# The last gate columns and the fifth chunk's second turn behind the down group, with fixed places for the late gates

## The chip, the core and the metric

The kernel runs on one core of a Trainium2 chip. The engines named here are PE (matrix products, written to PSUM banks), DVE and ACT (work on tiles of 128 rows), POOL, and SP, which here issues nearly all transfers. Each engine works through its own queue in order and waits where an operand is not yet there. The metric is the time of one execution on the device in microseconds (us); the time of the kernel before is the median of its runs, 891.66 us (891.43 to 891.97).

## The reference, cut to what matters

The input is a sequence of 256 rows of width 1024. Two layers follow, each of them a feed-forward part (FFN), a mixer and a second FFN; the first layer's mixer is a convolution module, the second's a latent attention (MLA). All of it is in 32-bit floats.

```
def swiglu_ffn(h, w1, w3, w2):
    return (jax.nn.silu(h @ w1) * (h @ w3)) @ w2          # w1, w3: 1024 x 2816, w2: 2816 x 1024

for i in range(DEPTH):                                     # DEPTH = 2
    h = h + 0.5 * swiglu_ffn(rmsnorm(h, ffn_norm1[i]), ffn1_w1[i], ffn1_w3[i], ffn1_w2[i])
    h = h + mixer(rmsnorm(h, mix_norm[i]))                 # conv module, then MLA
    h = h + 0.5 * swiglu_ffn(rmsnorm(h, ffn_norm2[i]), ffn2_w1[i], ffn2_w3[i], ffn2_w2[i])
return rmsnorm(h, final_norm)
```

There are thus four FFNs, called FFN0 to FFN3 below, and they run one after the other with the mixers between them: FFN0, conv, FFN1, FFN2, MLA, FFN3.

## The kernel before, in words

**Products in three parts.** A 32-bit product is made of three products in a faster format: each operand is split into a high part (a rounded copy, made by ACT for weights: `hi`, L248 and L216) and a low part (what is left, made by DVE: `lo`, L249 and L202), and PE adds hi·lo, hi·hi and lo·hi into one bank (`mm3`, L334, L337, L338). One such product of 128 x 128 by 128 x 512 starts about every 0.227 us on PE.

**Weights.** The weights come as raw blocks of 1 MB (128 x 2048) through SP's queue, in the order in which they are used (L240 for most, L225 and L182 for those loaded ahead of a mixer or of the next FFN). Four raw buffers take turns, so a load starts once the block four places earlier has been split by both ACT and DVE. Each block is split in two halves (128 x 1024). Five buffers hold the split blocks.

**An FFN, up part.** The gate columns are made in chunks: five chunks of 512 columns of w1 and w3 and a sixth, half as wide, whose w1 and w3 columns lie in one block (`both` in the code, c = 5). A chunk's products `u` stand in four PSUM banks of tag A (two for each half of the 256 rows, tb = 0, 1); the sixth chunk has two. ACT takes the Silu of the w1 products (L1005), DVE multiplies by the w3 products (L1011) and gives `s`, which is silu(h w1) · (h w3) for 128 rows and 512 columns. The fourth chunk is made by a scheme of seven products in place of eight ("seven"), with added and subtracted blocks.

**The turn of the gates.** The down product needs the gates with the columns on the partitions. So each `s` is turned: DVE transposes it in 32 x 32 pieces (STREAM_TRANSPOSE, L505, `gt<-s`), SP writes it to memory in four transfers of 64 KB (L509, `gd<-gt`), and reads it back with one of 256 KB (L514, `gb<-gd`); ACT then makes the high half Gh (L890; L881 for the last columns) and DVE the low half Gl (same lines). `turn` does so for chunks 0 to 4, `turn_last` for the sixth chunk, whose two halves share one tile.

**The down part.** The 22 column blocks of the gates are used in pairs, so w2 has 11 blocks, counted 0 to 10. Blocks 0 to 3 are used by a second group of seven products (`seven_products`, with casts L216 and L202, sums L260 and forms L367/L370), then blocks 4 to 8 one after another (`Rows.block`, each 24 products for all four output banks), and the last two in `Rows.finish`, bank by bank. Where the FFN is followed by a norm that is turned by transfers (`apart`: FFN1 and FFN2), `finish` takes the last three, blocks 8 to 10. The gates of the last columns belong to blocks 9 and 10 and those of the fifth chunk to blocks 8 and 9.

**Hand-over.** As each output bank is done, DVE adds it to h (L826). From FFN0 to conv the norm's scaled rows `hn` (L707, L708) are transposed on PE (`tp`, L473); from FFN1 to FFN2 and from FFN2 to MLA the rows of h are turned by transfers like the gates (`hd<-rows` L509, `rows<-hd` L514) and then split into Xh (ACT, L625) and Xl (DVE, L626).

**What sets the order.** The program is written in the order of the code, and a scheduler places each engine's instructions by priority; `urgent` raises it, and `order(a, b)` puts a behind b with no wait of its own where both are on one engine. So a call of `order` between instructions of one engine fixes their places in its queue. `casts[n, i]` is the pair (hi, lo) of half i of the n-th block; `n_used[0]` counts the blocks used; `last_turn[0]` is the latest transpose; `gates` lists the pairs (Gh, Gl).

Of the kernel before, what the change touches and what calls it, by code (L numbers as in the profile page):

```python
# [19 lines left out]
P = 128  # L20
# [69 lines left out]
def trunk(ctx: ExitStack, tc: tile.TileContext, x, xt, first, pos, invf, gfin, wdw,  # L90
# [283 lines left out]
    def seven_products(xh, xl, forms, banks, late={}, ahead=False):  # L374
# [30 lines left out]
        kept = tmp.tile([P, 512], F32, tag="s", name=uid("p5"))  # L405
# [376 lines left out]
    class Rows:  # L782
# [6 lines left out]
        def seven(self, forms, late):  # L789
            seven_products(self.zh, self.zl, forms, self.o, late)  # L790
# [17 lines left out]
        def finish(self, rh, make_next, act, apart=False):  # L808
# [62 lines left out]
    def ffn_in(act, X, make_next, beside, apart, seven_up, seven_down):  # L871
        down_sums, first_form = [], {}
# [55 lines left out]
        for c in range(6):  # L928
# [18 lines left out]
            for m in range(0 if u else 1 if both else 2):  # L947
# [4 lines left out]
                for tb in range(NT):  # L952
                    u[m, tb] = bank("A", "u")
# [42 lines left out]
            if both:  # L996
                last_s = tmp.tile([P, 512], F32, tag="s", name=uid("s"))
            for tb in range(NT):
                if both:
                    s = last_s.rearrange("p (f t c) -> p t f c", t=NT, c=P)[:, tb]  # L1000
                    ug, uu = (u[0, tb][:, v].rearrange("p (f c) -> p f c", c=P) for v in (slice(w), slice(w, 2 * w)))
                else:
                    s = tmp.tile([P, 512], F32, tag="s", name=uid("s"))
                    ug, uu = u[0, tb], u[1, tb]
# [5 lines left out]
                mul = urgent(nc.vector.tensor_mul) if c in seven_up or c + 1 in seven_up else nc.vector.tensor_mul  # L1010
                mul(s, s, uu)  # L1011
                if not both:
                    turn(c, tb, w, s)
        o = Rows(Gh, Gl, NF, make_next is Final, seven_down)
        if seven_down:
            both = (xp.tile([P, KT, S], F32R, tag=tag, name=uid("rows")) for tag in ("Xh", "Xl"))
            late = {2: None, 3: None}
            o.seven({**first_form, **forms_of(down_sums[1:], *both, late)}, late)
            turn_last(last_s)
            for gate in gates[-NT - 2:]:  # L1020
                for ins, cast in zip(gate, casts[n_used[0] + 1, 0]):
                    order(ins, cast.ins)
        stage.append("down")
        for i in range(4 if seven_down else 0, NF // 2 - (3 if apart else 2)):
            beside()
            o.block(i)
            beside()
# [876 lines left out]
```

## Time and profile before

| What | us |
|---|---|
| median of the runs (lowest, highest) | 891.66 (891.43, 891.97) |
| the profiled execution, its own time | 891.0 |
| its span in the profile | 889.1 |
| PE busy | 881.5 (99%) |
| DVE busy | 768.7 (86%) |
| ACT busy | 580.2 (65%) |
| POOL busy | 104.8 (12%) |

Times in the rows are counted from the span's start. A row of a timeline has the start, the duration, the engine, the line, the operation, the output and the inputs by tile name, the shape, the count where neighbours of one kind are drawn together, and in brackets how long the engine sat idle before and what ended that. SPq rows are the times at which SP issues a transfer; a tile's answer has the time from issue to landing (least, median, most). The windows about the down parts' ends (busy time of each engine, its instructions, the granted clock as a share, the share of the transfer engines that was in use, GB/s) are:

```profile
core 0: us, PE busy (x) PEld busy (x) DVE busy (x) ACT busy (x) POOL busy (x), PEclk, DMA share, GB/s
143.00:181.00 38.00, 38.00 (x174) 31.54 (x172) 30.50 (x51) 30.85 (x68) 0.95 (x3) 1.00 0.83 307
405.00:446.00 41.00, 41.00 (x183) 33.95 (x182) 29.93 (x34) 22.30 (x32) 1.18 (x4) 1.00 0.88 327
579.00:620.00 41.00, 41.00 (x183) 33.95 (x182) 29.81 (x34) 22.35 (x31) 0.95 (x3) 1.00 0.83 305
840.00:884.00 44.00, 43.15 (x202) 36.04 (x200) 28.67 (x34) 21.30 (x31) 1.48 (x5) 1.00 0.43 165
```

They are FFN0, FFN1, FFN2 and FFN3 in this order.

### The profile page before, as it was taken

The page shows a single profiled execution, that of the slowest core. Times are in us where ns is not written, and L with a number is a line of the kernel's source. Part 1 is how long each engine was busy: PE and PEld are TensorE (multiplying, and loading weights), DVE is VectorE, ACT ScalarE, POOL GpSimd, SP SyncE. Part 2 cuts the span into 40 slices and gives each one's busy share as a digit, 9 for nine tenths or more (in the row PEclk, how much of TensorE's full clock was granted, in tenths as well). Part 3 has the DMA queues.
Part 4 walks back from the last instruction along what each step waited for, and adds up shares of the span by engine and source line. Part 5 has one row for each costly group of instructions (what it writes and reads, how often), then busy time and mean ns, then how long its engine had stood idle before and what let it go on. Part 6 is the DMA issues. An engine that isn't in the chain of part 4 may idle for free.

```text
span 889.1 us, 12241 instructions
## 1 busy us (share of the span) xinstructions
PE 881.5 (99%) x4209; PEld 741.9 (83%) x4209; DVE 768.7 (86%) x1106; ACT 580.2 (65%) x1001; POOL 104.8 (12%) x227
## 2 busy tenths in 40 slices
PE   9999999999999999999999999999999999999997
PEld 7888887898988888888888888888899888888886
DVE  6899999789999899989598999995778679999873
ACT  7667858789887656647385465673777666563762
POOL 1000000079952000000010000001400010000000
PEclk9999999999999999999999999999999999999999
DMA  9884929834216945929859278396644558387451
GB/s 336 302 312 148 390 84 354 330 137 148 96 60 230 328 188 204 360 83 358 293 191 335 93 259 308 116 394 200 224 144 142 190 171 334 99 324 257 160 218 48
DMA packets 68174, 198.94 MB, mean 224 GB/s; under 512 B 7952, under 2 KB 38544, under 8 KB 48784
## 3 DMA queue, kind: packets, MB, share of 16 engines
q1 hardware_dynamic: 67680, 197.47, 62.4%
q8 instruction: 33, 0.54, 0.2%
q10 hardware_dynamic: 432, 0.69, 0.2%
q14 instruction: 29, 0.24, 0.1%
HBM read 181.87 MB, written 16.25 MB: 223 GB/s over the span
## 4 chain that ended last, share of the span: by engine, by line
PE 97%; DVE 1%; ACT 0%; DMA 0%; issue 0%; ACTq 0%
PE u L338 17%; PE u L334 17%; PE u L337 17%; PE o L334 9%; PE o L338 9%; PE o L337 9%; PE u L1060 3%; PE gate L1060 3%; PE o L1296 3%; PE u L438 2%; PE sc L1657 1%; PE tp L473 1%; DVE lo L202 1%; PE pairs L1103 1%; PE a L337 1%; PE a L338 1%
## 5 line engine op out<-in xcount | busy, mean ns | idle before, releaser
L249 DVE TENSOR_TENSOR lo<-raw,hi 128x1024 fp32r<-128x1024 f32 (+1 forms) x228 | 267.0, 1212 | 25.8 <-ACT hi L248 25.2
L248 ACT CAST hi<-raw 128x1024 fp32r<-128x1024 f32 (+1 forms) x230 | 229.1, 1044 | 83.9 <-DMA raw<-in_f2w 31.5
L338 PE MATMUL u<-hi,Xl 128*128 128x512 f32 x592 | 230.4, 389 | 0.0
L337 PE MATMUL u<-hi,Xh 128*128 128x512 f32 x592 | 230.3, 389 | 0.0
L334 PE MATMUL u<-lo,Xh 128*128 128x512 f32 x592 | 229.8, 389 | 0.0
L216 ACT CAST hi<-raw 128x1024 fp32r<-128x1024 f32 x112 | 111.5, 1050 | 59.7 <-DVE raw L202 44.8
L202 DVE TENSOR_TENSOR lo<-raw,hi 128x1024 fp32r<-128x1024 f32 x112 | 132.1, 1216 | 2.5 <-ACT hi L216 2.4
L338 PEld LDWEIGHTS u<-hi,Xl 128*128 128x128 f32 x592 | 111.1, 188 | 23.5 <-DVE Xl L492 0.5
L337 PEld LDWEIGHTS u<-hi,Xh 128*128 128x128 f32 x592 | 111.1, 188 | 23.1
L334 PEld LDWEIGHTS u<-lo,Xh 128*128 128x128 f32 x592 | 111.1, 188 | 23.0
L337 PE MATMUL o<-hi,Gh 128*128 128x512 f32 (+1 forms) x276 | 106.5, 386 | 0.0
L338 PE MATMUL o<-hi,Gl 128*128 128x512 f32 (+1 forms) x276 | 106.5, 386 | 0.0
L334 PE MATMUL o<-lo,Gh 128*128 128x512 f32 (+1 forms) x276 | 106.2, 387 | 0.0
L464 POOL TENSOR_TENSOR ms<-ss 128x1 f32<-128x1 f32 x16 | 8.1, 510 | 592.6 <-ACT junk L456 592.6
L202 DVE TENSOR_TENSOR raw<-raw,raw 128x2048 f32<-128x2048 f32 x32 | 73.2, 2288 | 2.4 <-DMA raw<-in_f1w 1.2
L334 PEld LDWEIGHTS o<-lo,Gh 128*128 128x128 f32 x276 | 51.8, 188 | 10.7 <-DVE lo L202 0.2
L337 PEld LDWEIGHTS o<-hi,Gh 128*128 128x128 f32 x276 | 51.8, 188 | 10.4
L338 PEld LDWEIGHTS o<-hi,Gl 128*128 128x128 f32 x276 | 51.8, 188 | 10.4
L1005 ACT ACTIVATE s<-u,R 128x512 f32<-128x512 f32 (+1 forms) x48 | 30.6, 647 | 36.3 <-PE u L338 35.4
L1149 DVE SCALAR_TENSOR_TENSOR acc<-V,dw,acc 128x128 f32<-128x128 f32 (+1 forms) x174 | 53.9, 392 | 0.0
L1170 ACT ACTIVATE prod<-V,dw 128x128 f32<-128x128 f32 (+1 forms) x128 | 45.6, 415 | 1.8 <-POOL Y L1171 1.0
L826 DVE SCALAR_TENSOR_TENSOR h<-o,rh,h 128x512 f32<-128x512 f32 (+1 forms) x18 | 13.0, 720 | 27.2 <-PE o L338 27.2
(271 smaller groups left out, 1303.8 us busy)
## 6 DMA issues: line engine op xcount, KB each, us to landing
raw<-in_f2w SPq DMA_DIRECT2D x66, 1024.0 KB, 6.0
raw<-in_f1w SPq DMA_DIRECT2D x62, 1024.0 KB, 7.0
raw<-in_cw SPq DMA_DIRECT2D x12, 1024.0 KB, 6.2
gd<-gt SPq DMA_DIRECT2D x176, 64.0 KB, 3.8
gb<-gd SPq DMA_DIRECT2D x28, 256.0 KB, 3.3
rows<-gd SPq DMA_DIRECT2D x16, 256.0 KB, 3.0
raw<-in_wo SPq DMA_DIRECT2D x4, 1024.0 KB, 4.8
hd<-rows SPq DMA_DIRECT2D x56, 64.0 KB, 2.3
```

The source lines that it names most:

```text
L202: ins = nc.vector.tensor_sub(out, left, right)
L216: casts[n, i] = nc.scalar.copy(hi[:, c], raw[:, c]), sub(lo[:, c], raw[:, c], hi[:, c].bitcast(F32))
L248: casts[len(loaded), i] = (nc.scalar.copy(hi[:, c], raw[:, c]), low.tensor_sub(lo[:, c], raw[:, c], hi[:, c].bitcast(F32)))
L249: low.tensor_sub(lo[:, c], raw[:, c], hi[:, c].bitcast(F32)))
L334: mm = nc.tensor.matmul(o, ah, bl, start=start, stop=False, skip_group_check=seeded)
L337: nc.tensor.matmul(o, ah, bh, start=False, stop=False, skip_group_check=seeded)
L338: return nc.tensor.matmul(o, al, bh, start=False, stop=stop, skip_group_check=seeded)
L1005: silu = nc.scalar.activation(s, ug, AF.Silu, scale=X.r[tb])
L1060: mm = nc.tensor.matmul(u[:, t], w[:, c], X.x[:, k, t], start=(k == 0), stop=(k == KT - 1))
L1149: dve_last.append(nc.vector.scalar_tensor_tensor(out if j == j1 - 1 else y, v, w, y, op0=ALU.mult, op1=ALU.add))
L1170: prods_last.append(nc.scalar.activation(p, v, AF.Copy, scale=w))
L1296: p = nc.tensor.matmul(o[tb, d], (Zl if kind == "x" else Zh)[:, f, tbs(tb)], (lo if kind == "l" else hi)[:, c], start=(f, kind) == (0, "l" ...
```

## The change

1. The sixth chunk's products `u` go to banks of tag B in place of A.
2. The sixth chunk's Silus, products and turn, and the fifth chunk's second turn (c = 4, tb = 1), are written behind the down part's seven group. Their places are fixed: the fifth chunk's second transpose behind the lo of block 4, the Silus behind the hi of block 4, the products behind the lo of block 5, and block 6's lo behind the last transpose.
3. The gates of the last four turns are ordered behind the second half of block 5's casts (before: those of the last columns and the three ahead of them behind block 5's first half), and the last two gates, on ACT and on DVE, behind block 7's casts and ahead of block 8's.
4. `kept`, the copy of the second product in the seven group, uses the rows tile of the first sum instead of a tile of `tmp`.
5. In `finish` the first product of a bank is ordered behind the last product of the bank ahead of it.

The number of instructions on PE, DVE, ACT, POOL and SP stays as it was. The core of the diff:

```
-    def forms_of(sums, sh, sl, late={}):
+    def forms_of(sums, sh, sl, late={}, after=None):
...
+            if i == 0 and after is not None:
+                order(cast, after.ins)
...
-        kept = tmp.tile([P, 512], F32, tag="s", name=uid("p5"))
+        if kept is None:
+            kept = tmp.tile([P, 512], F32, tag="s", name=uid("p5"))
...
                         after = nxt.turned if i == 3 and a == 1 and rh is not None and not self.last else ()
+                        if rh is not None and i and a == 0:
+
+                            after = done,
...
         def turn_last(g):
 
             bv = turn_blocks(act, g, 4, "g", ())
-            order(last_turn[0], casts[n_used[0], PIECES - 1][1].ins)
...
-                    u[m, tb] = bank("A", "u")
+                    u[m, tb] = bank("B" if both else "A", "u")
...
-            if both:
-                last_s = tmp.tile([P, 512], F32, tag="s", name=uid("s"))
-            for tb in range(NT):
...
-                silu = nc.scalar.activation(s, ug, AF.Silu, scale=X.r[tb])
-                if both and seven_down and tb == 0:
-                    load_to(n_used[0] + 3)
-                    for i in range(PIECES):
-                        order(casts[n_used[0] + 2, i][0], silu.ins)
...
+            for tb in range(0 if both else NT):
+                s = tmp.tile([P, 512], F32, tag="s", name=uid("s"))
+                nc.scalar.activation(s, u[0, tb], AF.Silu, scale=X.r[tb])
+                mul = urgent(nc.vector.tensor_mul) if c in seven_up or c + 1 in seven_up else nc.vector.tensor_mul
+                mul(s, s, u[1, tb])
+                if 2 * c + tb < 9:
+                    turn(c, tb, w, s)
                 else:
...
+                    late_turns.append((c, tb, w, s))
...
-            o.seven({**first_form, **forms_of(down_sums[1:], *both, late)}, late)
+            load_to(n_used[0] + 3)
+            o.seven({**first_form, **forms_of(down_sums[1:], *both, late, casts[n_used[0] + 2, 0][0])}, late, down_sums[0][1])
+
+            plain = n_used[0]
+            for t in late_turns:
+                turn(*t)
+                order(last_turn[0], casts[plain, PIECES - 1][1].ins)
+            last_s = tmp.tile([P, 512], F32, tag="s", name=uid("s"))
+            for tb in range(NT):
+                s = last_s.rearrange("p (f t c) -> p t f c", t=NT, c=P)[:, tb]
+                ug, uu = (u[0, tb][:, v].rearrange("p (f c) -> p f c", c=P) for v in (slice(w), slice(w, 2 * w)))
+                silu = nc.scalar.activation(s, ug, AF.Silu, scale=X.r[tb])
+                mul = nc.vector.tensor_mul(s, s, uu)
+                order(silu, casts[plain, PIECES - 1][0].ins)
+                order(mul, casts[plain + 1, PIECES - 1][1].ins)
             turn_last(last_s)
-            for gate in gates[-NT - 2:]:
-                for ins, cast in zip(gate, casts[n_used[0] + 1, 0]):
+            for i in range(PIECES):
+                order(casts[plain + 2, i][1], last_turn[0].ins)
+            for gate in gates[-4:]:
+                for ins, cast in zip(gate, casts[plain + 1, PIECES - 1]):
                     order(ins, cast.ins)
...
             o.block(i)
+            if seven_down and i == 6:
+
+                for gate in gates[-2:]:
+                    for k, ins in enumerate(gate):
+                        order(ins, casts[plain + 3, PIECES - 1][k].ins)
+                        for piece in range(PIECES):
+                            order(casts[plain + 4, piece][k], ins.ins)
             beside()
```

In the rows of the order that follow, tiles have buffer numbers. DVE in FFN1, the kernel before: `lo_3950` is block 4, then 3971, 3991, 4022, 4054, 4086 and 4118 are blocks 5 to 10, and `lo_4150` is the next FFN's first; `gt_4009`, `gb_4016` are the last turn.

```order
L249 TENSOR_TENSOR lo_3950<-raw_3948,hi_3949 128x1024 x2
L505 STREAM_TRANSPOSE gt_4009<-s_3854 128x512
L249 TENSOR_TENSOR lo_3971<-raw_3969,hi_3970 128x1024
...
L890 TENSOR_TENSOR Gl_2909<-gb_3773,Gh_2908 128x4x128
...
L249 TENSOR_TENSOR lo_3991<-raw_3989,hi_3990 128x1024 x2
L249 TENSOR_TENSOR lo_4022<-raw_4020,hi_4021 128x1024 x2
L249 TENSOR_TENSOR lo_4054<-raw_4052,hi_4053 128x1024 x2
L249 TENSOR_TENSOR lo_4086<-raw_4084,hi_4085 128x1024 x2
L249 TENSOR_TENSOR lo_4118<-raw_4116,hi_4117 128x1024 x2
L881 TENSOR_TENSOR Gl_2909<-gb_4016,Gh_2908 128x512
L249 TENSOR_TENSOR lo_4150<-raw_4148,hi_4149 128x1024 x2
```

DVE at the same place in the changed kernel: `lo_3932`, 3953, 3973, 4020, 4052 are blocks 4 to 8; `gt_3991`, `gb_3998` are the fifth chunk's second turn, `gt_4007`, `gb_4014` the last one.

```order
L249 TENSOR_TENSOR lo_3932<-raw_3930,hi_3931 128x1024 x2
L508 STREAM_TRANSPOSE gt_3991<-s_3762 128x512
L249 TENSOR_TENSOR lo_3953<-raw_3951,hi_3952 128x1024 x2
L1026 TENSOR_TENSOR s_4002<-s_4002,u_3792 128x2x128
L1026 TENSOR_TENSOR s_4002<-s_4002,u_3793 128x2x128
...
L895 TENSOR_TENSOR Gl_2908<-gb_3758,Gh_2907 128x4x128
L508 STREAM_TRANSPOSE gt_4007<-s_4002 128x512
L249 TENSOR_TENSOR lo_3973<-raw_3971,hi_3972 128x1024 x2
L249 TENSOR_TENSOR lo_4020<-raw_4018,hi_4019 128x1024 x2
L895 TENSOR_TENSOR Gl_2908<-gb_3998,Gh_2907 128x4x128
L886 TENSOR_TENSOR Gl_2908<-gb_4014,Gh_2907 128x512
L249 TENSOR_TENSOR lo_4052<-raw_4050,hi_4051 128x1024 x2
```

The last transpose moved from behind block 4's lo to behind block 5's lo, the two products and two gates, and the last gate from behind block 10's lo to ahead of block 8's. (Of the two gates between the products and the last transpose one is left out, as are two of three gates in the rows of before.) ACT has the casts in the same places as DVE its low halves. SP in FFN1, before:

```order
L509 DMA gd_4011<-gt_4009 32x4x128 x4
L240 DMA raw_4084<-in_f2w 128x2048
L240 DMA raw_4116<-in_f2w 128x2048
L514 DMA gb_4016<-gd_4011 128x512
L240 DMA raw_4148<-in_f1w 128x2048
L240 DMA raw_4156<-in_f1w 128x2048
L240 DMA raw_4290<-in_f1w 128x2048
L182 DMA raw_4298<-in_f1w 128x2048
L182 DMA raw_4300<-in_f1w 128x2048
L182 DMA raw_4302<-in_f1w 128x2048
L509 DMA hd_4186<-rows_139 32x4x128 x4
```

And in the changed kernel, where `raw_4082` and `raw_4114` are blocks 9 and 10 and `raw_4146` onwards belong to the next FFN:

```order
L512 DMA gd_3993<-gt_3991 32x4x128 x4
L240 DMA raw_4082<-in_f2w 128x2048
L512 DMA gd_4009<-gt_4007 32x4x128 x4
L517 DMA gb_3998<-gd_3993 128x512
L240 DMA raw_4114<-in_f2w 128x2048
L240 DMA raw_4146<-in_f1w 128x2048
L517 DMA gb_4014<-gd_4009 128x512
L240 DMA raw_4154<-in_f1w 128x2048
L240 DMA raw_4288<-in_f1w 128x2048
L182 DMA raw_4296<-in_f1w 128x2048
...
L512 DMA hd_4184<-rows_139 32x4x128 x4
```

Two turns of gates now stand between the loads, and the last one's `gb` follows the loads of block 10 and of the next FFN's first block. (Two more L182 loads stand ahead of `hd`, left out here.)

More of the change, by code (lines that the diff above doesn't have):

```diff
@@ L372, in forms_of, with seven_products @@
         return out
-    def seven_products(xh, xl, forms, banks, late={}, ahead=False):
+    def seven_products(xh, xl, forms, banks, late={}, ahead=False, kept=None):
         def rows(a, tb):
@@ L787, in __init__, with seven @@
             self.seeded = seeded
-        def seven(self, forms, late):
-            seven_products(self.zh, self.zl, forms, self.o, late)
+        def seven(self, forms, late, kept):
+            seven_products(self.zh, self.zl, forms, self.o, late, kept=kept)
         def mm(self, part, i, tb, d, o, f0, f1, o0=0, o1=512, after=(), after_last=()):
@@ L871, in ffn_in @@
     def ffn_in(act, X, make_next, beside, apart, seven_up, seven_down):
-        down_sums, first_form = [], {}
+        down_sums, first_form, late_turns = [], {}, []
         Gh = act.tile([P, NF, S], F32R, tag="Gh", name=uid("Gh"))
@@ L995, in ffn_in @@
                     beside()
-            if both:
-                last_s = tmp.tile([P, 512], F32, tag="s", name=uid("s"))
-            for tb in range(NT):
-                if both:
-                    s = last_s.rearrange("p (f t c) -> p t f c", t=NT, c=P)[:, tb]
-                    ug, uu = (u[0, tb][:, v].rearrange("p (f c) -> p f c", c=P) for v in (slice(w), slice(w, 2 * w)))
-                else:
-                    s = tmp.tile([P, 512], F32, tag="s", name=uid("s"))
-                    ug, uu = u[0, tb], u[1, tb]
-                silu = nc.scalar.activation(s, ug, AF.Silu, scale=X.r[tb])
-                if both and seven_down and tb == 0:
-                    load_to(n_used[0] + 3)
-                    for i in range(PIECES):
-                        order(casts[n_used[0] + 2, i][0], silu.ins)
[L1010 to L1013, printed above, removed]
+            for tb in range(0 if both else NT):
[5 more added lines that the diff above has]
+                    turn(c, tb, w, s)
+                else:
+                    late_turns.append((c, tb, w, s))
         o = Rows(Gh, Gl, NF, make_next is Final, seven_down)
```

## The prediction, made before the changed kernel was run

> **What bounds the kernel now.** I read the page's first, second and fourth part, then the waits of PE, then the timelines of DVE, SP, ACT and PE around the change.
>
> ```profile
> PE 881.5 (99%) x4209; PEld 741.9 (83%) x4209; DVE 768.7 (86%) x1106; ACT 580.2 (65%) x1001; POOL 104.8 (12%) x227
> ...
> PEclk9999999999999999999999999999999999999999
> ...
> PE 97%; DVE 1%; ACT 0%; DMA 0%; issue 0%; ACTq 0%
> ```
>
> PE is busy for 881.5 of 889.1 us, always at the full granted clock, and the chain that ends last is PE for 97%. The change keeps every product, so it can win only what PE waits for:
>
> ```profile
> PE warm L326 <- DVE still L321: 1.0, 1, 1.0
> PE o L334 <- DVE lo L202: 0.4, 1, 0.4
> PE u L438 <- ACT Xh L667: 0.2, 1, 0.2
> ```
>
> The first of these is the start of the program and the third a norm, both untouched. The second lies in FFN0's seven products:
>
> ```profile
> 136.40 0.47 PE L334 MATMUL o<-lo,rows 128*128 128x512 f32 x1 [0.37 <-DVE lo L202]
> ```
>
> PE stands for 0.37 us, and this matmul takes 0.47 where its neighbours take 0.39: 0.45 in all. What an edit can lose is not bounded like that. So I looked at how late DVE and the loads may be. FFN1's down part, where the gates of the last columns arrive, reads so on DVE (start, duration, idle before in brackets):
>
> ```profile
> 407.71 0.71 DVE L505 STREAM_TRANSPOSE gt<-s 128x512 f32<-128x512 f32 x1
> ...
> 409.44 1.89 DVE L890 TENSOR_TENSOR Gl<-gb,Gh 128x512 fp32r<-128x512 f32 x3
> 411.25 8.03 DVE L249 TENSOR_TENSOR lo<-raw,hi 128x1024 fp32r<-128x1024 f32 x7
> 420.25 4.86 DVE L249 TENSOR_TENSOR lo<-raw,hi 128x1024 fp32r<-128x1024 f32 x4 [0.97 <-ACT hi L248]
> 425.02 0.68 DVE L881 TENSOR_TENSOR Gl<-gb,Gh 128x512 fp32r<-128x512 f32 x1
> ...
> 430.85 2.36 DVE L249 TENSOR_TENSOR lo<-raw,hi 128x1024 fp32r<-128x1024 f32 x2 [2.62 <-ACT hi L248]
> ```
>
> The last turn's transpose starts at 407.71, the low half of its gate is made at 425.02, and between them the two long rows alone hold eleven lo halves, one every 8.03/7 = 1.147 us. SP's queue shows why the gate is so late:
>
> ```profile
> 408.44 1.93 SPq L509 DMA_DIRECT2D gd<-gt  x4
> 412.49 2.62 SPq L240 DMA_DIRECT2D raw<-in_f2w  x2
> 415.79 0.33 SPq L514 DMA_DIRECT2D gb<-gd  x1
> 417.04 5.92 SPq L240 DMA_DIRECT2D raw<-in_f1w  x3
> 425.13 8.44 SPq L182 DMA_DIRECT2D raw<-in_f1w  x3
> 435.44 5.77 SPq L509 DMA_DIRECT2D hd<-rows  x8
> 441.37 1.54 SPq L514 DMA_DIRECT2D rows<-hd  x2
> ```
>
> The tile of the gate says how long its last DMA is under way there:
>
> ```profile
> DMA to landing us min/median/max: 6.4/6.4/6.4
> ```
>
> So the gate lands at 415.79 + 6.4 = 422.2, 14.5 us after the transpose began. A turn with nothing large in the queue, earlier in FFN0, is much shorter:
>
> ```profile
> 114.44 0.71 DVE L505 STREAM_TRANSPOSE gt<-s 128x512 f32<-128x512 f32 x1
> ...
> 118.33 0.34 SPq L514 DMA_DIRECT2D gb<-gd  x1
> ...
> DMA to landing us min/median/max: 2.7/2.7/2.8
> ```
>
> It takes 118.33 + 2.7 - 114.44 = 6.6 us. The turn's length is thus set by the 1 MB loads ahead of it.
>
> **The change, part by part.** (a) The last columns' u goes into B banks, which are free there; two Silus, two products, and the last turn go behind the seven group, and the fifth chunk's second turn takes the last turn's old place. Ahead of the lo that PE waited for, DVE has two products and one transpose less. Gain: the 0.45 above. It can't be more, as PE waits nowhere else for this, nor below zero unless B's banks are held: nothing else asks for one in that stretch. I take -0.45. The two products and Silus move to where DVE and ACT have work, not PE: nothing by themselves, hidden by PE's down products; what they cost is lateness, counted in (c). `kept` in the rows tile and the ordered products bank by bank change no instruction's size and leave the same matmuls; from the 0.37 above as the nearest stall I bound these between -0.2 and +0.4 and take 0.
>
> (b) The last transpose comes later. In its old place now stands the fifth chunk's second; then follow two lo halves (2.3 us), the two products (each half the size of the 0.68 gate row: 0.7 together), two gates (1.89 x 2/3 = 1.26) and only then the last transpose. With the first transpose (0.63 from start to start) that is 4.9 us; the three instructions gone ahead give back up to 1.3. So 3.6 to 4.9 later; I take 4.2, 411.9 in FFN1.
>
> (c) The gates are pinned: both last ones now stand on ACT and DVE between the casts of block 7 and those of block 8 (counted in the down weights from 4), where the last gate before stood behind the casts of block 10. Both engines run their queue in order, so the six hi and six lo halves of blocks 8 to 10 wait for the landing, and SP's next loads for them. With as many loads ahead of gb as before (two), the turn takes 14.5 us again: landing at 411.9 + 14.5 = 426.4. Bounds: 418.5 on an empty queue (6.6 us) and 429.0 with one load more (two issues of loads take 2.62 on SP). I take 426.4, since the order leaves two loads ahead of the gate as the row has. Then ACT casts the gate and block 8, at these rows' pace:
>
> ```profile
> 423.57 0.61 ACT L881 CAST Gh<-gb 128x512 fp32r<-128x512 f32 x1
> 424.78 2.00 ACT L248 CAST hi<-raw 128x1024 fp32r<-128x1024 f32 x2 [0.61 <-DMA raw<-in_f1w]
> ```
>
> The first lo half is done 0.6 + 1.0 + 1.15 = 2.75 us after the landing, the sixth 5 x 1.147 later, at 426.4 + 8.5 = 434.9. PE needs the first half of block 8 and the last of block 10, and then the next FFN's Xh, at these points:
>
> ```profile
> 429.56 0.39 PE L334 MATMUL o<-lo,Gh 128*128 128x512 f32 x1
> ...
> 432.96 0.39 PE L334 MATMUL o<-lo,Gh 128*128 128x512 f32 x1
> ...
> 445.88 0.39 PE L334 MATMUL u<-lo,Xh 128*128 128x512 f32 x1
> ```
>
> 429.15 is in time, 434.9 is 1.9 late. FFN1 and FFN2 finish with three blocks bank by bank, so each loses 1.9 (0 if it lands by 424.5, 4.5 at the upper bound). FFN0 lands earlier, by its own rows:
>
> ```profile
> 142.44 0.71 DVE L505 STREAM_TRANSPOSE gt<-s 128x512 f32<-128x512 f32 x1
> ...
> 150.89 0.34 SPq L514 DMA_DIRECT2D gb<-gd  x1
> ...
> DMA to landing us min/median/max: 3.6/3.6/3.6
> ...
> 159.80 2.36 DVE L249 TENSOR_TENSOR lo<-raw,hi 128x1024 fp32r<-128x1024 f32 x2 [0.50 <-ACT hi L248]
> ...
> 174.87 0.75 DVE L826 SCALAR_TENSOR_TENSOR h<-o,rh,h 128x512 f32<-128x512 f32 x1 [0.76 <-PE o L338]
> 177.61 0.49 DVE L708 TENSOR_SCALAR hn<-h,R 128x512 f32<-128x512 f32 x1 [2.00 <-POOL R L467]
> ...
> 178.75 1.03 PE L473 MATMUL tp<-ident,hn 128*128 128x128 f32 x8
> ```
>
> Its turn takes 150.89 + 3.6 - 142.44 = 12.1; landing 142.44 + 4.2 + 12.1 = 158.7. It finishes block by block (24 matmuls of 0.227, 5.4 us a block), so I put the direct wait at 0 (at most 0.4). FFN3 has nothing to load behind it and DVE idles 9.38 us there, so 0:
>
> ```profile
> 872.23 0.75 DVE L826 SCALAR_TENSOR_TENSOR h<-o,rh,h 128x512 f32<-128x512 f32 x1 [9.38 <-PE o L338]
> ```
>
> (d) What the held engines pass on. While ACT and DVE stand, no raw buffer comes free, so SP stops too, and the loads bunch ahead of the next norm.
> FFN0 to conv: block 10's lo ends at 158.7 + 8.5 = 167.2, before at 162.2, so DVE is 5.1 behind. It makes up the 0.76 before an add and some 0.7 in smaller pockets; 0.65 lies between hn (178.10) and PE's transposes; the 2.00 is a wait for POOL, which itself follows the adds and moves along. Leaves 3.0. The second 128 rows pass the same way once more: between 0 and 2.0, I take 1.0. Together 4.0 (0 to 7).
> FFN1 to FFN2: five 1 MB loads that had left SP from 417.04 to 433 now leave as buffers come free, the last after the fifth pair of lo halves: 430.3 + 4 x 2.3 = 439.5, and hd stands behind it in SP's queue. The row had hd at 435.44; with PE's 1.9 it would be 437.4, so 2.1 late, and each landing goes from the turn's quick 2.7 to 6.4, 3.7 more. Spare is what SP shows between the first 128 rows' last landing (435.44 + 1.4 for the issues of four + 2.7 = 439.5) and 441.37, 1.8. Leaves 4.0, as Xh has no room:
>
> ```profile
> 444.09 1.28 ACT L625 ACTIVATE Xh<-rows,G 128x128 fp32r<-128x128 f32 x4 [0.45 <-DMA rows<-hd]
> ...
> 616.14 1.28 ACT L625 ACTIVATE Xh<-rows,G 128x128 fp32r<-128x128 f32 x4 [2.02 <-DMA rows<-hd]
> ...
> 619.96 0.39 PE L334 MATMUL a<-lo,Xh 128*128 128x512 f32 x1
> ```
>
> FFN2 to MLA has 619.96 - 617.4 = 2.5 there where FFN1 has 0.5, so 4.0 falls to 2.0; with loads that may have drained by then I take the middle, 1.0 (0 to 2.0). Bounds of FFN1's: 0 to 5.8, with no spare.
>
> **The sum.** -0.45 + FFN0 4.0 + FFN1 (1.9 + 4.0) + FFN2 (1.9 + 1.0) = +12.35. On the profiled run's 891.0 us (889.1 span and 1.9 around it) that is 903.35; that run lies 0.66 under the median of the runs, 891.66, so 904.0 for a median.
>
> PEclk reads 9 in all 40 slices, with no PE wait longer than 1.0 inside. [...]
>
> **Rivals.**
> R1, the other side: the gate lands before the queue reaches it. DVE comes to the gates about 417; if the turn takes its empty-queue 6.6 us (landing 418.5), or anything up to 424.5, PE's wait is 0 and only (a) is left: 891.66 - 0.45 = 891.2. For it: SP has loads held back too, so fewer are ahead. Against: the row's 14.5 and 12.1 have the same loads ahead. It decides at a turn of 12.6 us, with (d) gone as well only near 10. Chance 0.13.
> R2: the lateness compounds. With the upper bounds in FFN1 and FFN2 (4.5 rather than 1.9 each) and the same hand-overs, +17.55: 909.2. For it: hd and gb wait twice each in the same queue. Chance 0.12.
> R3: the hand-overs hold (loads drain while PE waits), only the direct waits stay, or the reverse: +3.35 gives 895.0, or +8.55 gives 900.2. For it: the hand-overs rest on the least certain step, the spare in SP's queue; against: Xh had 0.5 us of room. Chance 0.15.
> R4: one wait crosses into a lower clock, which PE's rows would show by 0.453 us from matmul to matmul instead of 0.227. If it stays low for as long as the longest wait was, 4.0, that is nine matmuls 0.227 later each: 906.0. For it: only that wait's length; against: the 9s of PEclk. Chance 0.03. [...]
>
> **How the numbers follow.** My case holds 0.57, its own range 900 to 907. The range reaches to the lower of R3 and most of R2: 895 to 910; R1 and the ends are left out. A difference of 0.2% (1.8 us) is about what can be told from none: R1 is within it in the main (0.12), 0.02 for something faster than PE's waits let me see, 0.86 slower.
>
> **What would show it.** PE's waits: the 0.4 for L202 gone (a); in its place o waiting for lo L249 near 431 to 437 and 615, 0.4 to 0.5 at a time (c); tp or hn near 180 (d); u waiting for Xh after 446. DVE and ACT should show an idle of 5 to 9 us ended by the DMA gb<-gd in each FFN, and SP a gap of like length with loads bunched behind. Wrong if the idle is under 3 us, or if it is there and PE doesn't wait: then a cover is longer than I read it.

## The result, and the profile after

The changed kernel takes 913.71 us (median; 911.81 to 914.64) where the kernel before takes 891.82: a ratio of 1.0243 (95% interval 1.0231 to 1.0256), 21.9 us slower. The direction was forecast, the time was not: 904.0 with a range of 895 to 910.

The page of the changed kernel, its first and fourth part, and then the waits of PE (us in total, times, longest):

```profile
PE 891.6 (98%) x4209; PEld 745.3 (82%) x4209; DVE 768.4 (84%) x1106; ACT 583.1 (64%) x1003; POOL 104.1 (11%) x227
...
PE 75%; DMA 9%; DVE 8%; ACT 4%; issue 2%; SPq 1%; POOL 0%; DVEq 0%; ACTq 0%; POOLq 0%
```

```profile
PE u L334 <- ACT Xh L628: 4.2, 1, 4.2
PE o L334 <- DVE lo L249: 3.4, 12, 1.2
PE a L334 <- ACT Xh L628: 3.3, 1, 3.3
PE tp L476 <- DVE hn L711: 2.8, 1, 2.8
```

PE, which before carried 97% of the chain, carries 75% of it: the rest runs through transfers, DVE and ACT. The waits are the four kinds that the prediction named: lo of the late blocks (c), and the three hand-overs to conv (tp), FFN2 (u) and MLA (a) (d). The wait for lo L202 is gone (a). The four add up to 13.7 us, while the profiled execution's span grew from 889.1 to 912.7, by 23.6. PE is also *busy* for 10.1 us more on the same 4209 products. ACT has two instructions more than before (1003, before 1001), though the change was described as adding none; they come up again below.

DVE in FFN1's down part (compare the rows from 407.71 of before):

```profile
415.19 0.70 DVE L508 STREAM_TRANSPOSE gt<-s 128x512 f32<-128x512 f32 x1
...
419.92 0.70 DVE L508 STREAM_TRANSPOSE gt<-s 128x512 f32<-128x512 f32 x1
420.55 4.59 DVE L249 TENSOR_TENSOR lo<-raw,hi 128x1024 fp32r<-128x1024 f32 x4
428.64 0.69 DVE L895 TENSOR_TENSOR Gl<-gb,Gh 128x512 fp32r<-128x512 f32 x1 [3.51 <-ACT Gh L895]
434.22 0.69 DVE L886 TENSOR_TENSOR Gl<-gb,Gh 128x512 fp32r<-128x512 f32 x1 [4.89 <-ACT Gh L886]
435.17 10.31 DVE L249 TENSOR_TENSOR lo<-raw,hi 128x1024 fp32r<-128x1024 f32 x9 [0.26 <-ACT hi L248]
```

The last transpose starts 419.92 - 415.19 = 4.73 us behind the place it had, which the fifth chunk's second one now takes. DVE then makes blocks 6 and 7 and stands for 8.4 us in two pieces for the two gates; nine lo halves follow without a pause. SP's queue in the same place shows the loads stopping with it, from 427.51 to 437.56:

```profile
425.17 0.33 SPq L240 DMA_DIRECT2D raw<-in_f1w  x1
427.51 0.33 SPq L517 DMA_DIRECT2D gb<-gd  x1
437.56 2.60 SPq L240 DMA_DIRECT2D raw<-in_f1w  x2
...
447.93 8.07 SPq L512 DMA_DIRECT2D hd<-rows  x8
```

The products behind a hand-over step slowly. PE's timeline at FFN1's end, and then the windows behind the hand-overs to conv, to FFN2 and to MLA (their columns as in the table of before; the granted clock stands ahead of the DMA share):

```profile
459.57 0.79 PE L334 MATMUL u<-lo,Xh 128*128 128x512 f32 x1 [4.20 <-ACT Xh L628]
460.16 0.63 PE L337 MATMUL u<-hi,Xh 128*128 128x512 f32 x1
460.59 0.63 PE L338 MATMUL u<-hi,Xl 128*128 128x512 f32 x1
```

```profile
183.00:187.00 4.00, 3.35 (x13) 2.86 (x14) 3.62 (x17) 3.05 (x10) 0.08 (x1) 0.67 0.76 289
...
459.00:462.00 3.00, 2.43 (x6) 1.95 (x7) 1.24 (x4) 2.88 (x6) 1.02 (x4) 0.50 0.46 134
462.00:465.00 3.00, 3.00 (x10) 2.38 (x9) 2.39 (x6) 3.00 (x7) 0.00 (x0) 0.63 0.69 175
643.00:646.00 3.00, 2.85 (x12) 2.36 (x13) 2.86 (x8) 3.00 (x9) 1.22 (x4) 1.00 0.41 118
```

From 460.16 to 464.0 a product starts every 0.43 us rather than every 0.227, and the granted clock is 0.50 and 0.63. It is low after the wait of 2.85 at conv too (0.67), though not after the 3.25 ahead of MLA (1.00).

Where the time went, by stages. A stage is told by the starts of PE's products in each timeline (for instance the down part of FFN1 from the first o to the first u of FFN2, 388.8 to 445.9 before), in us:

| Stage | before | changed | fixed place taken out (e1) | fixed place alone (e2) | one block earlier (e10) |
|---|---|---|---|---|---|
| FFN0 down, to tp | 56.5 | 60.5 | 55.9 | 56.6 | 64.9 |
| tp to conv's first gate | 2.2 | 4.0 | 2.3 | 3.3 | 4.0 |
| conv | 90.8 | 91.6 | 90.8 | 91.4 | 92.0 |
| FFN1 up | 117.0 | 117.0 | 117.0 | 117.0 | 117.0 |
| FFN1 down, to u | 57.1 | 63.3 | 57.5 | 58.5 | 61.2 |
| FFN2 up | 117.0 | 119.3 | 117.6 | 117.6 | 117.6 |
| FFN2 down, to a | 57.1 | 64.3 | 57.1 | 58.0 | 63.2 |
| MLA and FFN3 up | 205.8 | 205.9 | 205.8 | 205.9 | 205.9 |
| FFN3 down, to the last product | 57.2 | 57.2 | 57.2 | 57.2 | 62.9 |

The changed kernel loses 17.4 us in three down parts, 1.7 from tp to conv's first gate and 2.3 in FFN2's up part (the two stretches with slow products) and 0.9 in conv; the down part of FFN0 began 0.9 later besides, as it did by 0.3 to 1.2 in other kernels here.

One thing in the description of the kernel is to be set right: the last columns' gates are used by block 10 alone; blocks 8 and 9 use the fifth chunk's. The times of the steps don't rest on it.

### The profile page after: what moved, and what is told of

Read it like the earlier page. It is cut to its first block, busy times and chain, and to the rows that moved or that the text cites. A ratio compares the mean times of both kernels' runs of the same rounds, so it can differ in the third digit from the quotient of the medians.

```text
span 912.7 us, 12228 instructions
## 1 busy us (share of the span) xinstructions
PE 891.6 (98%) x4209; PEld 745.3 (82%) x4209; DVE 768.4 (84%) x1106; ACT 583.1 (64%) x1003; POOL 104.1 (11%) x227
## 4 chain that ended last, share of the span: by engine, by line
PE 75%; DMA 9%; DVE 8%; ACT 4%; issue 2%; SPq 1%; POOL 0%; DVEq 0%; ACTq 0%; POOLq 0%
PE u L334 15%; PE u L337 14%; PE u L338 14%; PE o L338 4%; PE o L334 4%; PE o L337 4%; PE gate L1079 3%; PE u L1079 3%; ACT hi L248 3%; DMA gd<-gt 3%; DVE lo L249 3%; PE u L441 2%; PE o L1315 2%; DMA gb<-gd 2%; DVE lo L202 2%
## 5 line engine op out<-in xcount | busy, mean ns | idle before, releaser
L249 DVE TENSOR_TENSOR lo<-raw,hi 128x1024 fp32r<-128x1024 f32 (+1 forms) x228 | 266.1, 1209 | 19.9 <-ACT hi L248 19.6
L202 DVE TENSOR_TENSOR lo<-raw,hi 128x1024 fp32r<-128x1024 f32 x112 | 132.3, 1216 | 5.7 <-ACT hi L216 5.7
L338 PEld LDWEIGHTS u<-hi,Xl 128*128 128x128 f32 x592 | 111.7, 189 | 23.6 <-DVE Xl L495 0.5
L334 PE MATMUL o<-lo,Gh 128*128 128x512 f32 (+1 forms) x276 | 108.3, 394 | 3.5 <-DVE lo L249 3.4
L202 DVE TENSOR_TENSOR raw<-raw,raw 128x2048 f32<-128x2048 f32 x32 | 73.2, 2288 | 4.1 <-DMA raw<-in_f2w 2.7
L1189 ACT ACTIVATE prod<-V,dw 128x128 f32<-128x128 f32 (+1 forms) x128 | 48.1, 418 | 3.3 <-POOL Y L1190 1.6
L1190 POOL TENSOR_TENSOR odd<-odd,prod 128x128 f32<-128x128 f32 (+1 forms) x62 | 33.8, 549 | 0.1
L895 ACT CAST Gh<-gb 128x512 fp32r<-128x512 f32 x24 | 14.4, 618 | 29.8 <-DMA gb<-gd 29.8
```

Source lines behind the costliest of these rows:

```text
L202: ins = nc.vector.tensor_sub(out, left, right)
L249: low.tensor_sub(lo[:, c], raw[:, c], hi[:, c].bitcast(F32)))
L334: mm = nc.tensor.matmul(o, ah, bl, start=start, stop=False, skip_group_check=seeded)
L338: return nc.tensor.matmul(o, al, bh, start=False, stop=stop, skip_group_check=seeded)
L1189: prods_last.append(nc.scalar.activation(p, v, AF.Copy, scale=w))
L1190: pool_last.append(nc.gpsimd.tensor_tensor(o, o, p, op=ALU.add))
```

## The experiments

**The fixed place of the last two gates taken out.**

```
-            if seven_down and i == 6:
-                for gate in gates[-2:]:
-                    ...
```

> The changed kernel without the fixed place of the last two gates: the scheduler now puts the fifth chunk's gate behind block 9's casts and the last gate one or two blocks behind block 10's, with the late turn, the B banks and the bank order kept. Theory (the place ahead of block 8 together with the late turn costs the time): ACT and DVE find the gates landed, PE's waits on lo L249, hn and Xh go, the 0.4 on lo L202 stays away: 891.0 to 892.5 us. Rival A (the late turn alone costs it, by its transfers among the loads): still over 900. Rival B (bank order or banks): still over 900.

Measured: 891.79 us, ratio 1.0003 (0.9993 to 1.0013). PE's waits of that kernel, but for the 1.0 us at the program's start:

```profile
PE u L334 <- ACT Xh L628: 0.2, 1, 0.2
```

The four kinds of wait are gone with these few lines, but for 0.2 us at FFN2's first product, and with them the 22 us; the later turn, the B banks, the bank order and `kept` are all still there. Rivals A and B fall.

**The fixed place alone, in the kernel before.**

```
+            plain = n_used[0]
...
             o.block(i)
+            if seven_down and i == 6:
+                for gate in gates[-1:]:
+                    for k, ins in enumerate(gate):
+                        order(ins, casts[plain + 3, PIECES - 1][k].ins)
+                        for piece in range(PIECES):
+                            order(casts[plain + 4, piece][k], ins.ins)
```

> The kernel before with one edit: its last gate is placed ahead of block 8's casts; the turn stays where it was. Theory: the gate lands at 422.2 in FFN1, so the sixth lo half ends at 422.2 + 8.5 = 430.7, 2.3 ahead of PE's need: no wait of PE on lo L249 in any FFN. ACT and DVE stand about 5 us, loads bunch, and the hand-overs lose 0 to 2 us each: 892 to 897. Rival A (the place alone does all of it, wherever the turn stands): 908 or more. Rival C (the place costs nothing, only the late turn does): 891.7, with no idle of ACT on the gate.

Measured: 897.45 us, ratio 1.0063 (1.0048 to 1.0079): 5.8 slower, a little over what was expected. DVE in FFN1, and then PE's waits:

```profile
426.41 0.69 DVE L881 TENSOR_TENSOR Gl<-gb,Gh 128x512 fp32r<-128x512 f32 x1 [6.66 <-ACT Gh L881]
```

```profile
PE u L334 <- ACT Xh L625: 1.3, 1, 1.3
...
PE a L334 <- ACT Xh L625: 0.7, 1, 0.7
PE tp L473 <- ACT hn L707: 0.4, 1, 0.4
```

DVE stands 6.7 us for the gate, and PE waits for no lo of a late block, as worked out; what it loses are hand-overs, 0.4 to 1.3 us each, in place of 2.8 to 4.2, and 1.7 between tp and the end of conv (the table's second and third row), where the clock stayed at 1.00. Together with the run above this makes a square: late turn alone +0.2, place alone +5.8, both +21.9. Most of the price is in the two together. The square isn't exact, since this run places one gate and the changed kernel two. Rivals A and C fall.

**The gates one block later, two blocks later, one block earlier.** One edit with three values: the two gates behind blocks 8's and 9's casts, behind 9's and 10's, and both behind block 6's.

```
-            if seven_down and i == 6:
+            if seven_down and i == 7:
...
-                for gate in gates[-2:]:
+                for n, gate in enumerate(gates[-2:]):
                     for k, ins in enumerate(gate):
-                        order(ins, casts[plain + 3, PIECES - 1][k].ins)
+                        order(ins, casts[plain + 4 + n, PIECES - 1][k].ins)
                         for piece in range(PIECES):
-                            order(casts[plain + 4, piece][k], ins.ins)
+                            order(casts[plain + 5 + n, piece][k], ins.ins)
```

> The changed kernel with its last two gates placed one behind block 8's and one behind block 9's casts (each ahead of the next block's). Theory: with the late turn landing 13.6 to 15.6 us after its transpose, only block 10's halves wait for the last gate, in FFN1 until about 434 - 7.5 = 426.5 on the clock of before, done by 429.5, PE needs them at 432.3: no wait on lo L249. Loads are held about 3 us less than in the changed kernel; hand-overs lose 0 to 3 each: 891 to 897. Rival A (late turn alone): over 900.

> The changed kernel with the last two gates placed behind block 9's and block 10's casts, in every FFN ahead of what follows. Theory: as without a fixed place, nothing waits, and what is left is the gain at FFN0's lo L202: 891.0 to 891.8, not told from before. If the place behind block 10 is late enough in FFN2 too, PE waits for neither lo nor Xh.

> The changed kernel with its last two gates one block earlier still: behind block 6's casts and ahead of block 7's. Theory: eight hi and lo halves wait for the same landing instead of six, 2 x 1.147 = 2.3 us more behind it in each FFN; PE's waits on lo L249 grow by about 2 in FFN0, FFN1 and FFN2, hand-overs by 0 to 1 each, FFN3 may begin to wait: 919 to 926. Rival (it is enough that both engines stand once; the place doesn't count): 912 to 915.

Measured: one later 894.91 us, ratio 1.0034 (1.0022 to 1.0047); two later 891.42, ratio 0.9994 (0.9986 to 1.0003); one earlier 919.45, ratio 1.0307 (1.0291 to 1.0323). So by the place of the first of the two gates, behind block 6, 7, 8 or 9, the price is +27.8, +21.9, +3.3 and -0.3. All three lie in what was expected. PE's waits one block earlier:

```profile
PE o L334 <- DVE lo L249: 12.9, 4, 4.0
PE tp L476 <- DVE hn L711: 2.2, 1, 2.2
PE a L334 <- ACT Xh L628: 1.3, 1, 1.3
PE u L334 <- ACT Xh L628: 1.3, 1, 1.3
```

They don't grow evenly, as had been expected they would: the direct wait goes from 3.4 to 12.9, and the hand-overs fall. That DVE and the loads catch up while PE itself is stopped in the middle of the down part fits this, but wasn't measured by itself. And FFN3, which the changed kernel left untouched, loses 5.7 us there. The direct waits were forecast to grow by about 2 in each of three FFNs and the hand-overs to grow a little; that the time still lies in the range is in part luck. The kernel with the gates two blocks later keeps everything else of the change, and PE waits nowhere in it (only the program's first 1.0 us are listed); it can't be told from the kernel before. In the one with the gates one block later, 1.9 of the 3.3 us lie between tp and the end of conv (94.9 us, before 93.0).

**The late turns issued by POOL in place of SP.**

```
-            dma = nc.sync.dma_start(dv[i], ...)
+            dma = (nc.gpsimd if late else nc.sync).dma_start(dv[i], ...)
...
-        last_read[0] = nc.sync.dma_start(b[:, :w], d)
+        last_read[0] = (nc.gpsimd if late else nc.sync).dma_start(b[:, :w], d)
```

> The changed kernel with the transfers of its last two turns (four gd and one gb each) issued by POOL instead of SP; the gates' place is kept. Theory (the turn is long because its transfers land in order behind the 1 MB loads of SP's queue): the last turn takes 6 to 10 us instead of 13.6 to 15.6, it lands 5 us earlier, PE's waits on lo L249 go and the hand-overs fall to less than half: 893 to 901. Rival (the transfers share what moves the bytes, whoever issues them): turn as long as now or longer, 911 to 918.

Measured: 913.86 us, ratio 1.0244 (1.023 to 1.0258). My theory of the turn falls. FFN1's last turn there, from DVE's and POOL's timelines and the tile gb:

```profile
420.60 0.71 DVE L508 STREAM_TRANSPOSE gt<-s 128x512 f32<-128x512 f32 x1
...
430.06 0.55 POOL L517 DMA_DIRECT2D gb<-gd  x1 [2.20 <-DMA gd<-gt]
...
DMA to landing us min/median/max: 4.5/4.5/4.5
```

The turn takes 430.06 + 4.5 - 420.60 = 14.0 us, on SP it took 427.51 + 6.0 - 419.92 = 13.6. The two lengths agree though SP's queue holds none of it any more. In FFN0 and FFN2 the last turn takes 13.4 and 13.5 where on SP it took 14.4 and 15.6, far from the 6 to 10 that were expected; PE's waits for lo L249 fall from 3.4 to 1.7, and the total stays, with the granted clock now low at all three hand-overs. So the last turn beside 1 MB loads is long here whether POOL issues it (13.4 to 14.0 us) or SP (13.6 to 15.6); that its transfers stand behind the loads in one queue explains at most a small part. That both share what moves the bytes fits this, but wasn't measured by itself.

**The next FFN's three loads left behind the norm's turn at FFN1's end.**

```
-                raw_to(len(loaded) + RAW_BUFS - self.by_dram)
+                raw_to(len(loaded) + (0 if self.by_dram else RAW_BUFS))
```

> The changed kernel, but at FFN1's end the three loads for the next FFN that are issued ahead of the norm's turn (L182) are left to be issued later, behind it. Theory (the held loads bunch ahead of hd and make Xh late): hd leaves and lands earlier, PE's 4.2 us for Xh falls under 2, the clock stays up there, 3 to 6.5 us less than the changed kernel, of which later blocks may take back some. Rival E (Xh is late because DVE's adds and transposes are late): the wait stays within 1 us of 4.2.

Measured: 922.86 us, ratio 1.0347 (1.0333 to 1.0361). The edit takes hold at FFN2's end too, where the norm is turned in the same way. Half right: PE's wait at FFN2's first product falls from 4.2 to 0.45, and the one at MLA's from 3.3 to 0.4, as they should if the loads held back are what makes Xh late. But what came later took back more than all of it (FFN2's up part takes 125.6 us, before 117.0; MLA and FFN3's up part 213.4, before 205.8):

```profile
469.57 1.99 ACT L248 CAST hi<-raw 128x1024 fp32r<-128x1024 f32 x2 [3.65 <-DMA raw<-in_f1w]
471.47 2.44 ACT L628 ACTIVATE Xh<-rows,G 128x128 fp32r<-128x128 f32 x8
```

ACT now waits 3.65 us for a weight, the second 128 rows' Xh stands behind it, and PE waits 4.1 us for that and the granted clock falls to 0.51. Loads ahead of the turn delay the first rows, loads behind it the second.

**Filled waits.** PE gets products of a still tile (results unused) where it would only wait: at FFN2's first products, and then at all three hand-overs.

```
+                if n == 0 and X.by_dram:
+                    last = keep_warm(24, after=down_mm[0])
```

> The changed kernel with 24 products of a still tile (128 x 256, bf16, results unused) on PE between FFN1's last product and FFN2's first, where PE waited 4.2 us for Xh. Theory (the granted clock falls after that wait, and the slow products behind it cost 2.5 us): the clock reads 1.00 behind FFN1, matmuls there step 0.227 us, and the time falls by 2 to 2.7 us against the changed kernel. Rival D (the slower products there are held by something else, such as loads or late weights): time and steps as in the changed kernel, within 0.5 us.

> The changed kernel with products of a still tile (128 x 256, bf16, results unused) on PE at all three hand-overs where PE waited for 2.8 us or more: 22 ahead of FFN0's transposes, 24 ahead of FFN2's first products and 24 ahead of MLA's. Theory (about 4 us of the loss are slow products behind those waits): the granted clock reads 1.00 in every stretch behind a hand-over and the time is 3 to 4.5 us less than that of the changed kernel run beside it. Rival (the waits and not the clock hold all of the loss): within 1 us of it.

> The changed kernel as it is, beside the one with the filled hand-overs on the same chip: 912 to 914.5 by its runs so far, with a granted clock of 0.5 to 0.7 for some 3 us behind two or three of the hand-overs.

Measured: filled at one place 913.07 us (907.84 to 915.73), ratio 1.0230 (1.0201 to 1.0259). The clock behind FFN1 reads 1.00 in all windows from 430 to 470, as expected. The total doesn't show it, since in the profiled execution the clock fell at the hand-over to MLA instead, where the changed kernel's had not. Filled at all three, 912.08 (910.83 to 912.42), ratio 1.0223 (1.0209 to 1.0237); the changed kernel beside it 913.95 (911.63 to 917.31), ratio 1.0256 (1.0236 to 1.0276). The windows behind the three hand-overs, filled and then not:

```profile
183.00:187.00 4.00, 3.58 (x27) 2.89 (x25) 3.31 (x14) 2.27 (x6) 1.01 (x3) 1.00 1.02 383
...
460.00:464.00 4.00, 3.01 (x12) 2.17 (x12) 1.23 (x5) 3.55 (x9) 1.26 (x4) 1.00 0.44 130
...
644.00:648.00 4.00, 4.00 (x23) 3.49 (x22) 4.00 (x9) 3.87 (x12) 0.00 (x0) 1.00 0.45 134
```

```profile
183.00:187.00 4.00, 2.57 (x10) 2.40 (x11) 3.10 (x13) 1.96 (x5) 0.76 (x2) 0.68 0.96 367
...
462.00:465.00 3.00, 3.00 (x10) 2.33 (x9) 1.17 (x5) 3.00 (x7) 0.00 (x0) 0.61 0.40 103
...
644.00:648.00 4.00, 4.00 (x11) 3.07 (x11) 4.00 (x11) 4.00 (x10) 0.00 (x0) 0.50 0.45 111
```

The clock stays up, but the median falls by 1.9, not 3 to 4.5: the products behind the waits are on time (the stage from tp to conv's first gate is 2.4 instead of 3.9, FFN2's up part 117.6 instead of 118.7, MLA and FFN3's up part 205.9 instead of 208.4), and conv gives 1.25 back where PE, come earlier, waits 1.3 for Xp. Ahead of that Xp stands a load of a function table on ACT:

```profile
195.24 1.28 ACT L1098 ACT_TABLE_LOAD   x1
...
196.71 0.62 ACT L723 ACTIVATE Xp<-tp,G 128x128 f32<-128x128 f32 x2
...
197.12 1.15 PE L1089 MATMUL gate<-Xp,raw 128*128 128x128 f32 x7 [1.29 <-ACT Xp L723]
```

The two intervals overlap, so the size of the saving isn't settled; that the clock falls because of these waits is shown by its staying up.

## Why the prediction was right and wrong

The sum was -0.45 + 4.0 + 5.9 + 2.9 = 12.35. The terms, with what the profiled execution shows. For a wait the bracketed idle time stands first; "in all" is measured from start to start against a step of 0.227 us, so it holds what PE takes to get going again (0.27 more at 620.99, which waited 1.19 and cost 1.46: the product starts 1.35 late, and the next one 0.11 more):

```profile
620.99 0.50 PE L334 MATMUL o<-lo,Gh 128*128 128x512 f32 x1 [1.19 <-DVE lo L249]
```

| Term | predicted | measured |
|---|---|---|
| (a) FFN0's wait for lo L202 | -0.45 | the wait is gone; with the gates late FFN0's down part is 0.6 to 0.7 shorter, but the time (891.42 to 891.79) can't be told from before |
| (b) last transpose later by | 4.2 | 4.73 |
| (c) turn in FFN0, FFN1, FFN2 | 12.1, 14.5, 14.5 | 14.4, 13.6, 15.6 |
| (c) PE for lo in FFN0 | 0 | 1.65 in all |
| (c) PE for lo in FFN1 | 1.9 | 1.8 in all |
| (c) PE for lo in FFN2 | 1.9 | 3.7 in all |
| (c) FFN3 | 0 | 0 |
| (d) FFN0 to conv | 3.0 + 1.0 | 3.0 in all at tp; behind it 1.7 to conv's first gate and 0.9 in conv |
| (d) FFN1 to FFN2 | 4.0 | 4.2 (4.4 in all) |
| (d) FFN2 to MLA | 1.0 | 3.3 (3.5 in all) |
| slow products behind u | 0 (R4: 2.0, chance 0.03) | 2.3, of which 1.65 by the clock |

The measured terms add up to 23.0 us. Less the 0.65 that FFN0 gains, and with 0.9 at the start and 0.4 in MLA and behind the last product, that is the span's 23.6. The mechanism was right: the gates placed ahead of block 8 stop both engines, the loads stop with them, and PE pays in the down parts and at three hand-overs; for most of the price it took both the late turn and the place. R1 was wrong because the landings came at turns of 13.6 to 15.6, never under 12.6. What failed is the size of five terms. Together they are 9.8 us short, and the time came 9.7 above the forecast:

1. *Behind FFN1's hand-over* (+2.3, put at nothing). FFN2's up part takes 119.3 us, and 117.6 where the wait was filled and the clock read 1.00 (e5 and e7): 1.65 is the price of the clock. The other 0.65 against the 117.0 of before are short waits for Xh and PE's starts behind them; they stand in e1 and e2 too. I gave R4 a chance of 0.03 because the row of PEclk held no fall; but it also held no wait of this length, so it was no evidence. Two of my own terms made single waits of 3.0 and 4.0 us, and the clock should have been worked into them. No run shows the step of 0.453 us that R4 takes, twice 0.227: the slow products start 0.43 us apart, at a granted clock of 0.50. Nor does the length of a wait decide the fall alone: the clock fell after waits of 2.15 and 2.6 (one block earlier) and 2.85 (the changed kernel), and stayed up after 2.3 and 3.25 in the same two runs (the last section has what was measured around them).
2. *FFN2 to MLA* (+2.5). I let the loads be drained by then. They weren't: hd's transfers there took up to 6.9 us to land against 3.8 before, and ACT waited 8.3 us for the rows against 2.0.
3. *FFN2's lo* (+1.8). Its landing came at 610.42 + 7.7 = 618.1, a turn of 15.6 rather than FFN1's copied 14.5, and the transpose 0.5 later than I took it; each of PE's six stops there costs some 0.27 more than the bracketed idle time. The upper bound of 4.5 held it.
4. *FFN0's lo* (+1.6). The turn was 14.4, not 12.1. And I let the lo halves follow each other at DVE's pace of 1.147 us. ACT's timeline says why they didn't:

```profile
161.39 0.62 ACT L886 CAST Gh<-gb 128x512 fp32r<-128x512 f32 x1 [6.94 <-DMA gb<-gd]
161.92 1.99 ACT L248 CAST hi<-raw 128x1024 fp32r<-128x1024 f32 x2
163.81 2.02 ACT L1779 ACTIVATE rows<-dpair,wpair 128x64 f32<-128x64 f32 x8
165.74 1.98 ACT L248 CAST hi<-raw 128x1024 fp32r<-128x1024 f32 x2
```

Conv's preparations stand between the casts in ACT's queue. Before, all but five of them had run by the time of the last gate (157.97), between casts that were early; behind the stop they come between casts that are late, and a block takes 3.8 us instead of 2.3.

5. *The second rows on the way to conv* (+1.6: 1.7 and 0.9 against 1.0). The clock is low here (0.67), but that isn't what the time goes by: from tp to the end of conv the changed kernel takes 95.6 us and before 93.0; filled, with the clock at 1.00, it takes 95.8, and the kernel with the gates one block later, whose clock stayed up too, 94.9. What these have in common is the two further instructions of ACT, two loads of a function table of 1.28 us each. A Sine (cc, L1474) now stands in ACT's queue behind the instruction that calls up the Sigmoid (sigm, L699), so ACT changes its table back and forth once more, at the hand-over. The kernels without the two loads (before, e1 and the gates two blocks later) take 93.0 to 93.1. No run takes out the loads alone, so how much of the 2.6 is theirs stays open.

The price of the turn was near for FFN1, though its reason was not: the transfers of a turn are about as slow from another queue (e9). That it came near is in part luck.

## What to carry to other kernels

An instruction put at a fixed place in an in-order queue takes all that stands behind it along with its operand's landing (in FFN1 the two gates held DVE for 8.4 us, and SP's loads from 427.51 to 437.56 with it): compare the landing, by rows of transfers made beside like loads, with the time at which the *next* instruction's user needs it, and place the late one behind everything that is ready before. When two edits are made together (a later producer and an earlier consumer), price them together; each alone cost 0.2 and 5.8 us here, both 21.9. Where a sum predicts single waits of 2 us or more on PE (the shortest that a fall of the clock followed here was 2.15), add to each the slower products that may follow it (1.65 and 2.5 us here). And where an edit moves work in ACT's queue, count the table loads of the two kernels (six and eight here, 1.28 us each) before pricing it.

## What the runs showed of the hardware that had not been expected

PE's granted clock fell to 0.50 after waits in the middle of a busy kernel, and the length of the wait alone doesn't tell when. In the changed kernel it fell after 2.85 and 4.20 and stayed up after 3.25. One block earlier it fell after 2.15, 2.6, 4.0 and 4.0 (PE's products take 0.63 us there in place of 0.39) and stayed up after 1.3, 1.3 and 2.3. In the changed kernel's trace the granted clock changes at 184.33, 187.74, 457.39, 464.22 and 911.37. These times lie 1, 79, 2 and 131 times 3.413 us apart, as if it were set by periods of that length; what sets it isn't shown. Of the period that ended at each of the two falls ahead of the kernel's end PE had stood for 2.7 us (to 184.33) and for 2.0 (to 457.39, busy for 1.39 of 3.42); of every other period at full clock up to the last product it stood for 1.8 or less, and the clock stayed up. One period at conv (the wait of 2.85) and two at MLA (the wait of 3.25) in the changed kernel, and then one at conv in the run with the loads left behind, whose wait there is 2.85 too:

```profile
180.92:184.33 3.41, 0.68 (x5) 0.58 (x6) 3.09 (x9) 1.22 (x3) 1.99 (x3) 1.00 0.98 380
...
638.30:641.71 3.41, 1.60 (x8) 0.98 (x6) 0.71 (x1) 0.00 (x0) 1.75 (x2) 1.00 0.37 89
641.71:645.13 3.42, 1.98 (x9) 1.62 (x10) 1.99 (x6) 2.43 (x6) 2.31 (x9) 1.00 0.60 188
```

```profile
180.98:184.40 3.42, 1.53 (x7) 0.94 (x5) 3.42 (x6) 0.72 (x2) 1.96 (x3) 1.00 1.02 426
```

In the first row PE stands for 2.7 of 3.41 us (it is busy for 0.68), and the clock falls at its end, 184.33. The wait of 3.25 is cut into 1.8 and 1.4 by a period's end, and the clock stays at 1.00; so it does in the last row, where the wait of 2.85 leaves 1.9 in the one period and 1.0 in the next. So two waits of 2.85 ended with a fall in one run and without in the other, and what differs in these rows is where they lie among the periods. The same program had both too: behind the hand-over to MLA the changed kernel's clock reads 1.00 in one execution (643 to 646) and 0.50 in another (644 to 648). In the changed kernel the clock stayed low for 3.41 us at conv, where PE was busy throughout, and for 6.83 behind FFN1's hand-over, where PE stood for 2.2 of the first 3.41. A fall cost 1.65 us behind FFN1's hand-over and, in the other execution of the changed kernel, 2.5 behind the one to MLA (208.4 against 205.9). With products without use in the three waits the windows behind them read 1.00.

A turn through memory (four transfers of 64 KB, then one of 256 KB) that takes 6.6 us with nothing large in the queue (FFN0, the kernel before) took 12.1 to 15.6 beside 1 MB loads on SP (both kernels), and 13.4 to 14.0 when POOL issued it.

A load of ACT's function table took 1.28 us each time in both kernels, and the order of ACT's queue goes with how often it came: six times in the kernel before, where the Sines stand ahead of the Sigmoids, eight in the changed one, where one falls behind.
